# First loads on one queue in the order of need, and x turned over inside the stream of context steps

## The chip, the cores and the metric

The kernel runs on one core of a Trainium2 chip. The metric is the device time of one execution in microseconds (us), the median of several runs. The engines are TensorE (PE, matrix products and transposes; its weight loads are shown as PEld), VectorE (DVE), ScalarE (ACT), GpSimd (POOL) and SyncE (SP, which here only issues transfers). Each engine takes its instructions strictly in the order in which the program was recorded, and waits at one until what it reads is there and the buffer that it writes is free.

## The reference, cut to what matters

The program is a transformer layer with a mixer (neighbourhood attention beside a bidirectional state-space scan) and 16 experts, followed by a second layer. The change touches only the start of the first layer: the modulation of the tokens `x` (512 x 1024) and of the context `ctx` (256 x 1024), and the projection of the context that the scan needs.

```python
def _modulate(x, g, shift, scale):
    return _rmsnorm(x, g) * (1 + scale) + shift

def _ada(cvec, w_ada, b_ada):
    mod = jax.nn.silu(cvec) @ w_ada + b_ada
    return jnp.split(mod, N_MOD, axis=-1)
...
    q, k, v, z, xbc, dt_raw, gates = _split_in(h @ w_in)
    qc, kc, vc, zc, xbcc, dtc, gates_c = _split_in(hc @ w_in)
...
    xbc = jax.nn.silu(_dwconv(xbc, conv_w, conv_b))
    xs, Bm, Cm = jnp.split(xbc, [SSD_WIDTH, SSD_WIDTH + SSD_GROUPS * SSD_STATE], axis=-1)
    dt_f = jax.nn.softplus(dt_raw[..., :SSD_HEADS] + dtb_f)
```

`w_ada` is 1024 x 6144 (25 MB). Shift and scale of the first modulation are its first 2048 columns (8.4 MB); the other 4096 columns are needed later only.

## The kernel before, in words

**Start.** Two queues issue the first loads. SP issues 16 pieces of `w_ada` (tiles `aw`, 512 KB each; eight buffers, so that the last eight wait for products with the first). ACT issues constants (`ident`, `va`, `vb`), then `ctx` and `x` in pieces of 128 rows. ACT squares and sums each row block, DVE scales all six blocks, PE turns them over (transposes, `xTp`), and ACT and DVE copy the results into `cT` (context) and `xT` (tokens), all before the last products with `w_ada` (`ada`, L695). From their sum come the columns `shc` and `gsc`, and `modulate` makes the modulated context as a sum of a rounded part and a rest (`c_hi`, `c_lo`), and later the same of the tokens (`h_hi`, `h_lo`).

**The stream.** A `Stream` object (`st`) holds units of work in a queue. A unit is a block of weight columns of `w_in`. Its raw pieces are loaded by SP into two buffers `raw`; each piece is split in pairs (`wh` by ACT at L200, `wl` by DVE or POOL at L220, five pairs alive at most). A step of a unit is one row block of weights: three products (L331 to L333) per output tile. Steps are counted, and `st.defer(n, f)` records `f` once n more steps are recorded. So the number of steps, not time, fixes where a piece of work stands in each engine's order.

**The order of units.** `ub` (B of the context, 32 steps in two halves of 16), `udt` (dt, 8 steps for the context and 8 for the tokens), then four units `xc` (32 steps each, the context's part of x in groups 0 to 3), then the q/k unit. After each half of a unit ACT starts a convolution (L760), DVE does the rest of it (L765, eight instructions), and after the unit ACT applies silu and the states of the context are made (L881 turns, L890 products).

**Beside the stream.** The other 4096 columns of `w_ada` come in 16 pieces of 1 MB (`ada_load2`, issued by ACT) and are multiplied one at a time (`ada_mm2`, L911), the first `ADA0` steps in, the next every `ADA` steps. The operations of dt (`dt_ops`) are deferred one per step: a turn of `dtT` on PE (L805, tile `dtn`), a softplus by polynomial on DVE, and `sums` (L812 to L814, tile `acs`) some steps later. PSUM tiles with the tag `m` share two banks in rotation: `dtn`, `acs`, one of the two turns of a group, the state products.

Of the kernel before, what the change touches and what calls it, by code (L numbers as in the profile page):

```python
# [9 lines left out]
F32 = mybir.dt.float32  # L10
# [564 lines left out]
ADA = 10  # L575
ADA0 = 20
# [15 lines left out]
AL = 8  # L592
SX = 56
# [19 lines left out]
def first_block(kb, es, after):  # L613
# [6 lines left out]
    S.dma_start(ident, A["ident"])  # L620
# [38 lines left out]
    S.dma_start(va, A["vec_a"])  # L659
    S.dma_start(vb, A["vec_b"])  # L660
    xT = p0.tile([128, 8, T], F32, name="xT")
# [3 lines left out]
    aw = {}  # L665

    def ada_load(kh):
        for j in range(4):
            t = p00.tile([128, 2, 512], F32, tag="aw", bufs=8, name="aw")
            nc.sync.dma_start(t, A["w_ada"][256 * kh:256 * kh + 256, 512 * j:512 * j + 512].rearrange("(k p) f -> p k f", p=128))  # L670
            aw[kh, j] = t

    ada_load(0)
    ada_load(1)
    xt = p00.tile([128, 6, D], F32, name="xt")
    for t in (4, 5, 0, 1, 2, 3):
        src = A["x"][128 * t:128 * t + 128] if t < 4 else A["ctx"][128 * (t - 4):128 * (t - 4) + 128]
        S.dma_start(xt[:, t], src)
# [13 lines left out]
    def ada_mm(kh):  # L692
        for k in range(2):
            for j in range(4):
                P.matmul(ada_ps[32 * j:32 * j + 32], sil[:, 2 * kh + k], aw[kh, j][:, k],  # L695
                         start=kh == 0 and k == 0, stop=kh == 3 and k == 1, skip_group_check=True)

    ss = p0.tile([128, 6], F32, name="ss")
    junk = xT[:, 0:2].rearrange("p a b -> p (a b)")
    for t in (4, 5, 0, 1, 2, 3):  # L700
        S.activation(junk, xt[:, t], AF.Square, accum_out=ss[:, t:t + 1])
    V.tensor_scalar(ss, ss, 1.0 / D, EPS, op0=ALU.mult, op1=ALU.add)
    rs = kb.rsqrt(ss, 6, p0)
    for t in (4, 5, 0, 1, 2, 3):
        V.tensor_scalar(xt[:, t], xt[:, t], rs[:, t:t + 1], None, op0=ALU.mult)
    ada_mm(0)
    ada_load(2)
    ada_mm(1)
    ada_load(3)
    S.dma_start(tri, A["tri"])  # L710
    S.dma_start(sel, A["sel"])
    for n in range(12):
        ps = PS.bank([128, 512], F32, "gsm"[n % 3], "xTp")
        for i in range(4):
            k, t = (2 * n + i // 2, 4 + i % 2) if n < 4 else (n - 4, i)
            P.transpose(ps[:, 128 * i:128 * i + 128], xt[:, t, 128 * k:128 * k + 128], ident)
        if n < 4:
            o, v = cT[:, 2 * n:2 * n + 2].rearrange("p a b -> p (a b)"), ps
        else:
            o, v = in_time(xT[:, n - 4]), ps.rearrange("p (r g c) -> p r g c", g=8, r=8)  # L720
        if n % 2:
            V.tensor_copy(o, v)
        else:
            S.activation(o, v, AF.Copy)
    ada_mm(2)
    ada_mm(3)
# [3 lines left out]
    def modulate(v, src, hi, lo, each):  # L730
# [62 lines left out]
    def dt_ops(t0, nt):  # L793
# [14 lines left out]
        def sums():  # L808
# [24 lines left out]
               ] + [None] * (16 if t0 else 38) + [  # L833
# [4 lines left out]
    udt = Unit([([(0, A["w_in"][:, ODT:ODT + 128])], 8)], 128)  # L838
# [17 lines left out]
    kb.group_b(udt, 0, act_t, T, ev_dtx)  # L856
    udt.steps = [(0, 2 * p + r, c, f) for p, r, c, f in udt.steps]
# [68 lines left out]
    ub = xbc_unit(OB, 16, bcT, b_nat)  # L926
    st.add(udt)
    us = [xc_unit(0)]
    st.pump_some(1)
# [1785 lines left out]
```

## Time and profile before

| | |
|---|---|
| Median of 3 runs | 3428.11 us (3427.95 to 3434.9) |
| The profiled execution's own time | 3432.32 us |
| Its span in the trace | 3430.5 us |
| PE busy | 3208.5 us (94%) |
| DVE busy | 1624.5 us (47%) |
| ACT busy | 1168.1 us (34%) |
| POOL busy | 554.2 us (16%) |
| First product of the stream (L331, `ub`) | 42.02 us into the span |
| First product of the q/k unit | 154.32 us into the span |

A line of the timeline gives the start, the duration, engine and line of the kernel, the instruction with what it writes and reads, how many were merged, and in brackets how long the engine had been idle and who released it. Durations of PE are modelled, so the distance from one start to the next says more. The shares over the whole span say little here: the change lies in the first 5% of it, and what matters is which engine is waited for there.

### The profile page before, as it was taken

The numbers are of one execution on the slowest core, as the hardware profiler recorded it, in microseconds if no ns is written. First come the engines' busy times: TensorE is split into PE (matmuls) and PEld (weight loads), VectorE is DVE, ScalarE is ACT, GpSimd is POOL, SyncE is SP. The second block draws the span as 40 slices with busy tenths as digits, with TensorE's granted clock in tenths as the row PEclk, the third lists the DMA queues.
The fourth block names the chain that finished last, engine by engine and source line by source line (L and its number), as shares of the span: only waits on it lengthen the run. The fifth ranks groups of instructions, "written<-read, shape, count | busy, mean of one in ns | idle before, by whom it ended". The sixth has DMA issues, their size and how long they took to land. (4 is left out here: it accounts for less than half of the span.)

```text
span 3430.5 us, 42023 instructions
## 1 busy us (share of the span) xinstructions
PE 3208.5 (94%) x16365; PEld 2207.9 (64%) x16365; DVE 1624.5 (47%) x3113; ACT 1168.1 (34%) x2064; POOL 554.2 (16%) x371
## 2 busy tenths in 40 slices
PE   7999999999899898888889888999999999999998
PEld 4778877777678543324324224777888877788887
DVE  5745557676554410111011015776544467765444
ACT  4455545555323100100000003555433355543332
POOL 2232213444110100000000000241111103401111
PEclk9999999999999899999999999999999999999999
DMA  8622122222444799999999996212323221123232
GB/s 293 237 65 79 59 79 79 83 80 77 146 147 184 310 410 418 420 421 421 421 421 421 421 421 227 68 47 71 93 92 105 92 88 56 41 84 99 92 92 80
DMA packets 223389, 646.64 MB, mean 188 GB/s; under 512 B 17973, under 2 KB 110253, under 8 KB 171349
## 3 DMA queue, kind: packets, MB, share of 16 engines
q1 hardware_dynamic: 211176, 607.26, 46.6%
q10 hardware_dynamic: 12013, 36.69, 3.0%
q8 instruction: 129, 2.11, 0.3%
q14 instruction: 71, 0.58, 0.0%
HBM read 628.67 MB, written 15.21 MB: 188 GB/s over the span
## 5 line engine op out<-in xcount | busy, mean ns | idle before, releaser
L1968 PE MATMUL hd<-xw,xe 128*64 128x512 f32 x2048 | 462.8, 595 | 63.1 <-DMA xw<-in_w_up_dram 42.1
L220 DVE TENSOR_TENSOR wl<-raw,wh 128x1024 fp32r<-128x1024 f32 (+1 forms) x306 | 377.9, 1249 | 124.3 <-ACT wh L200 122.8
L200 ACT ACTIVATE wh<-raw 128x1024 fp32r<-128x1024 f32 (+1 forms) x349 | 343.4, 1003 | 212.2 <-PE psg L333 133.1
L331 PE MATMUL psg<-HA,wh 128*128 128x512 f32 (+1 forms) x1024 | 392.6, 383 | 0.0
L332 PE MATMUL psg<-HB,wh 128*128 128x512 f32 (+1 forms) x1024 | 387.7, 379 | 3.9 <-DVE HB L467 3.9
L333 PE MATMUL psg<-HA,wl 128*128 128x512 f32 (+1 forms) x1024 | 388.0, 379 | 0.0
L1968 PEld LDWEIGHTS hd<-xw,xe 128*64 128x64 f32 x2048 | 151.6, 137 | 363.4 <-issue 241.2
L2009 PE MATMUL down<-xw,hidT 128*64 128x512 f32 x1024 | 237.8, 600 | 36.5 <-DMA xw<-in_w_down_dram 36.4
L331 PE MATMUL psg<-h_hi,wh 128*128 128x512 f32 x584 | 255.3, 437 | 1.1 <-DVE vsb L1334 0.9
L333 PE MATMUL psg<-h_hi,wl 128*128 128x512 f32 x584 | 236.9, 406 | 0.0
L332 PE MATMUL psg<-h_lo,wh 128*128 128x512 f32 x584 | 236.5, 405 | 0.0
L332 PEld LDWEIGHTS psg<-HB,wh 128*128 128x128 f32 x1024 | 195.0, 190 | 38.6 <-DVE HB L467 4.7
L333 PEld LDWEIGHTS psg<-HA,wl 128*128 128x128 f32 x1024 | 194.6, 190 | 35.9
L331 PEld LDWEIGHTS psg<-HA,wh 128*128 128x128 f32 x1024 | 195.7, 191 | 33.8
L2009 PEld LDWEIGHTS down<-xw,hidT 128*64 128x64 f32 x1024 | 75.0, 137 | 188.1 <-issue 120.6
L2627 POOL TENSOR_TENSOR va<-va,ga 128x512 f32<-128x512 f32 x44 | 90.9, 2066 | 546.1 <-DVE va L2609 546.0
L2024 ACT ACTIVATE yh<-down,gcol 128x512 fp32r<-128x512 f32 x16 | 11.0, 686 | 489.4 <-PE down L2009 489.4
L1980 DVE TENSOR_TENSOR hid<-hid,hd 128x512 f32<-128x512 f32 x32 | 22.0, 687 | 314.0 <-PE hd L1968 313.9
L2043 POOL TENSOR_TENSOR Y<-Y,R 128x512 f32<-128x512 f32 x4 | 5.0, 1275 | 966.4 <-ACT tmp L2041 966.4
L220 POOL TENSOR_TENSOR wl<-raw,wh 128x1024 fp32r<-128x1024 f32 (+1 forms) x43 | 101.7, 2368 | 291.2 <-ACT wh L200 291.2
L331 PE MATMUL psg<-wh,hidh 128*128 128x512 f32 x352 | 139.5, 396 | 0.0
L333 PE MATMUL psg<-wh,hidl 128*128 128x512 f32 x352 | 139.2, 396 | 0.0
(487 smaller groups left out, 5979.3 us busy)
## 6 DMA issues: line engine op xcount, KB each, us to landing
xw<-in_w_gate_dram SPq DMA_DIRECT2D x128, 1024.0 KB, 19.8
xw<-in_w_up_dram SPq DMA_DIRECT2D x128, 1024.0 KB, 19.8
xw<-in_w_down_dram SPq DMA_DIRECT2D x126, 1024.0 KB, 19.8
raw<-in_w_up_dram SPq DMA_DIRECT2D x176, 256.0 KB, 3.7
raw<-in_w_in_dram SPq DMA_DIRECT2D x34, 1024.0 KB, 5.2
raw<-in_w_in_dram SPq DMA_DIRECT2D x96, 256.0 KB, 3.1
raw<-in_w_down_dram SPq DMA_DIRECT2D x44, 512.0 KB, 4.3
raw<-in_w_in_dram SPq DMA_DIRECT2D x33, 512.0 KB, 4.7
```

What stands on the lines that cost most here:

```text
L200: nc.scalar.activation(wh[:, :kn, :nco], src, AF.Copy)
L220: eng.tensor_tensor(wl[:, :kn, :nco], src, wh[:, :kn, :nco].bitcast(F32), op=ALU.subtract)
L331: nc.tensor.matmul(ps, l, r, start=first, stop=False, skip_group_check=skip)
L332: nc.tensor.matmul(ps, l, rh, start=False, stop=False, skip_group_check=skip)
L333: nc.tensor.matmul(ps, lh, r, start=False, stop=last, skip_group_check=skip)
L1968: P.matmul(ps[c][64 * e:64 * e + 64], xe[p // 2][k // 2 % 2][:, 2 * (k // 4) + k % 2, c0:c0 + 64], self.tiles[p, w, k, e][:, 512 * c:512 * ...
L1980: V.tensor_tensor(acts[p, c], acts[p, c], ps[c], op=ALU.mult)
L2009: P.matmul(down[h][64 * e:64 * e + 64], b[:, 64 * e:64 * e + 64], w[:, 1024 * r + 512 * h:1024 * r + 512 * h + 512], start=j == 0 and r == ...
L2024: S.activation(hi, down[h], AF.Copy, scale=gates[p])
L2043: G.tensor_tensor(o, o, R3[:, :512], op=ALU.mult)
L2627: G.tensor_tensor(v, v, g[j], op=ALU.mult)
```

## The change

All first loads are issued by SP in one order: constants, the two blocks of `ctx`, eight pieces of `w_ada` (now one row block of 128 x 2048 each, 1 MB, six buffers), the first two pieces of `w_in`, and only then `x`. ACT issues no loads ahead of its first work. Only the context is normalised and turned over before the stream. The tokens are squared, scaled and turned over inside the stream: squares at steps 18 to 27, the row factors at 34, the scaling at 38 to 47, and eight turns (`x_turn`) at steps 54 to 89, each with a DVE instruction that modulates straight out of PSUM. The tokens' part of dt gets a unit of its own (`udtx`, whose weights are loaded and split a second time), and stands behind `xc` of group 1 instead of behind `ub`. The other pieces of `w_ada` start 48 steps in instead of 20 and follow every 8 steps instead of 10. The context's dt is deferred by 6 steps instead of 14. Half of the rests `c_lo` go to DVE instead of POOL. Nineteen products of `ident` with itself (`warm`) stand ahead of the stream.

```diff
-ADA = 10
-ADA0 = 20
+ADA = 8
+ADA0 = 48
-AL = 8
-SX = 56
+AL = 4
+SX = 8
...
+    xt = p00.tile([128, 2, D], F32, name="xt")
+    for t in range(2):
+        nc.sync.dma_start(xt[:, t], A["ctx"][128 * t:128 * t + 128])
+    aw = []
+
+    def ada_load(k):
+        aw.append(p00.tile([128, 4, 512], F32, tag="aw", bufs=6, name="aw"))
+        nc.sync.dma_start(aw[k], A["w_ada"][128 * k:128 * k + 128, :2048].rearrange("p (j f) -> p j f", f=512))
+
+    for k in range(6):
+        ada_load(k)
...
-    for t in (4, 5, 0, 1, 2, 3):
-        S.activation(junk, xt[:, t], AF.Square, accum_out=ss[:, t:t + 1])
...
+    def x_turn(k):
+
+        ps = PS.bank([128, 512], F32, "m", "xTp")
+        for t in range(4):
+            P.transpose(ps[:, 128 * t:128 * t + 128], xx[:, t, 128 * k:128 * k + 128], ident)
+        o = cT[:, 2 * (k % 4):2 * (k % 4) + 2].rearrange("p a b -> p (a b)")
+        V.tensor_scalar(in_time(o), ps.rearrange("p (r g c) -> p r g c", g=8, r=8), gsc[:, 0, k:k + 1], shc[:, 0, k:k + 1],
+                        op0=ALU.mult, op1=ALU.add)
+        S.activation(h_hi[:, k], o, AF.Copy)
+        (G if k % 2 else V).tensor_tensor(h_lo[:, k], o, h_hi[:, k].bitcast(F32), op=ALU.subtract)
...
-            (G if k % 2 or v else V).tensor_tensor(lo[:, k], src[:, k], hi[:, k].bitcast(F32), op=ALU.subtract)
+            (G if k % 2 else V).tensor_tensor(lo[:, k], src[:, k], hi[:, k].bitcast(F32), op=ALU.subtract)
...
-               ] + [None] * (16 if t0 else 38) + [
+               ] + [None] * (16 if t0 else 22) + [
...
-        spread(14, dt_ops(4, 2) + [lambda: tt(ddc, dtv[:, 4:6], dte[:, 4:6]),
+        spread(6, dt_ops(4, 2) + [lambda: tt(ddc, dtv[:, 4:6], dte[:, 4:6]),
...
+    kb.warm("m", 14)
...
-    for i in range(3):
-        ada_load2(i)
+    st.pump_some(1)
...
-    modulate(0, xT, h_hi, h_lo, lambda k: st.fill(1.0))
-    zero.close()
+    for i in range(3):
+        st.defer(26 + 6 * i, lambda i=i: ada_load2(i))
+    rx_ = []
+    for t in range(4):
+        st.defer(18 + 3 * t, lambda t=t: S.activation(junk, xx[:, t], AF.Square, accum_out=ss[:, t:t + 1]))
+        st.defer(38 + 3 * t, lambda t=t: by_r(xx[:, t], rx_[0][:, t:t + 1]))
+    st.defer(34, lambda: rx_.append(row_r(0, 4)))
+    for k in range(8):
+        st.defer(54 + 5 * k, lambda k=k: x_turn(k))
     for g in range(1, 4):
         us.append(xc_unit(g))
+        if g == 1:
+            st.add(udtx)
         st.finish(us[g - 1])
```

**How the order moves.** On ACT, from the end of the context's rounded parts (`c_hi`) to the convolution of `ub`'s second half (the second `bcT<-psc`), before:

```order
L737 ACTIVATE c_hi<-cT 128x256 x2
L950 ACT_TABLE_LOAD
L950 ACTIVATE alog<-alog 128x64
L737 ACTIVATE h_hi<-xT 128x512 x4
L200 ACTIVATE wh<-raw 128x1024
L760 ACTIVATE bcT<-psc,cols,cw 128x256 x2
L737 ACTIVATE h_hi<-xT 128x512
...
L737 ACTIVATE h_hi<-xT 128x512
L760 ACTIVATE bcT<-psc,cols,cw 128x256 x2
```

and in the changed kernel, with line numbers of that kernel:

```order
L959 ACTIVATE alog<-alog 128x64
L200 ACTIVATE wh<-raw 128x1024
L767 ACTIVATE bcT<-psc,cols,cw 128x256 x2
L964 ACTIVATE cT,ss<-xx 128x1024
L200 ACTIVATE wh<-raw 128x1024
L964 ACTIVATE cT,ss<-xx 128x1024
L200 ACTIVATE wh<-raw 128x1024
L964 ACTIVATE cT,ss<-xx 128x1024
L911 DMA aw_430<-in_w_ada_dram 128x2048
L964 ACTIVATE cT,ss<-xx 128x1024
L200 ACTIVATE wh<-raw 128x1024
L767 ACTIVATE bcT<-psc,cols,cw 128x256 x2
```

The eight rounded parts of the tokens are gone from here, and four squares of 1024 columns stand in their place. On DVE, from the second half's convolution of group 0 (`xc`) to the copy of the sums (`acs`), in the changed kernel (before, no turn of x stands here):

```order
L220 TENSOR_TENSOR wl<-raw,wh 128x1024
L730 TENSOR_SCALAR cT<-xTp,gsc,shc 128x8x8x8
L733 TENSOR_TENSOR h_lo<-cT,h_hi 128x512
L730 TENSOR_SCALAR cT<-xTp,gsc,shc 128x8x8x8
L772 SCALAR_TENSOR_TENSOR xc<-psc,cw,xc 128x255 x2
...
L772 SCALAR_TENSOR_TENSOR xc<-psc,cw,xc 128x254 x2
L220 TENSOR_TENSOR wl<-raw,wh 128x1024
L730 TENSOR_SCALAR cT<-xTp,gsc,shc 128x8x8x8
L733 TENSOR_TENSOR h_lo<-cT,h_hi 128x512
L730 TENSOR_SCALAR cT<-xTp,gsc,shc 128x8x8x8
L822 COPY acs<-acs 128x128
```

The third L730 is the modulation of turn 4. On PE, the sums stand one bank rotation behind that turn (turn 4, turn 5, sums, all with tag `m`), with the changed kernel's rows

```order
L919 MATMUL ada<-aw_582,sil 32x512 x4
...
L728 MATMUL xTp<-ident,xx 128x128 x4
...
L728 MATMUL xTp<-ident,xx 128x128 x4
L819 MATMUL acs<-n,tri 128x2x32
L820 MATMUL acs<-n,tri 128x2x32
L821 MATMUL acs<-n,tri 128x128
```

where before the sums followed products of `xc` alone, and seven pieces of `ada` and the tokens' dt products stood ahead of them. Now four pieces do (the last of them is shown), and the tokens' dt stands behind.

## Rows read from the trace of the kernel before

**Rows 1.** Busy time by stretch: us, then PE, PEld, DVE, ACT, POOL, PEclk, DMA, GB/s
```profile
58.00:76.60 18.60, 18.60 (x128) 13.92 (x124) 17.92 (x27) 8.93 (x14) 10.64 (x5) 1.00 0.50 170
94.50:125.00 30.50, 27.57 (x194) 20.38 (x194) 25.71 (x50) 12.38 (x17) 4.75 (x2) 0.94 0.75 257
125.00:154.30 29.30, 28.65 (x201) 21.54 (x202) 22.33 (x43) 16.72 (x24) 7.36 (x4) 1.00 0.68 245
```
**Rows 2.** Timeline from the last piece of w_ada to the stream's first product
```profile
35.37 1.90 PE L695 MATMUL ada<-aw,sil 128*32 128x512 f32 x10 [1.56 <-DMA aw<-in_w_ada_dram]
39.21 1.22 DVE L220 TENSOR_TENSOR wl<-raw,wh 128x1024 fp32r<-128x1024 f32 x1 [1.21 <-ACT wh L200]
41.05 1.05 DVE L732 TENSOR_SCALAR cT<-cT,gsc,shc 128x256 f32<-128x256 f32 x3
42.02 0.58 PE L331 MATMUL psc<-c_hi,wh 128*128 128x256 f32 x1 [3.31 <-ACT c_hi L737]
```
**Rows 3.** Transfers from 0 to 60 us: GB/s in 40 slices of 1.5 us, issues
```profile
GB/s 0 124 371 358 397 408 400 400 404 403 395 407 388 385 388 385 371 388 388 388 384 392 381 385 390 310 225 410 421 437 415 354 209 4 12 232 406 49 0 5
aw<-in_w_ada_dram SPq DMA_DIRECT2D x16, 512.0 KB, 7.6
aw<-in_w_ada_dram ACTq DMA_DIRECT2D x3, 1024.0 KB, 5.0
xt<-in_ctx_dram ACTq DMA_DIRECT2D x2, 512.0 KB, 6.9
```
**Rows 4.** Timeline of ACT: squares, first convolution taps, silu with table load, weight parts
```profile
14.27 1.06 ACT L701 ACTIVATE xT<-xt 128x1024 f32<-128x1024 f32 x1
15.45 1.06 ACT L701 ACTIVATE xT<-xt 128x1024 f32<-128x1024 f32 x1
58.87 1.00 ACT L760 ACTIVATE bcT<-psc,cols,cw 128x256 f32<-128x256 f32 x2
75.74 1.28 ACT L784 ACT_TABLE_LOAD   x1 [4.12 <-DVE bcT L765]
78.00 1.99 ACT L200 ACTIVATE wh<-raw 128x1024 fp32r<-128x1024 f32 x2
```
**Rows 5.** Timeline of DVE and POOL: row factors, scalings, convolution, dt, a POOL rest
```profile
20.59 0.17 DVE L702 TENSOR_SCALAR ss<-ss 128x6 f32<-128x6 f32 x1 [12.09 <-ACT xT L701]
23.00 4.07 DVE L705 TENSOR_SCALAR xt<-xt,rs_y 128x1024 f32<-128x1024 f32 x6
66.00 4.04 DVE L732 TENSOR_SCALAR xT<-xT,gsc,shc 128x512 f32<-128x512 f32 x2
67.18 2.57 POOL L220 TENSOR_TENSOR wl<-raw,wh 128x1024 fp32r<-128x1024 f32 x1
71.70 3.96 DVE L765 SCALAR_TENSOR_TENSOR bcT<-psc,cw,bcT 128x255 f32<-128x255 f32 x8
75.58 0.41 DVE L846 COPY dtT<-psg 64x256 f32<-64x256 f32 x1
85.64 0.62 DVE L829 SCALAR_TENSOR_TENSOR d<-d,u 128x128 f32<-128x128 f32 x2
```
**Rows 6.** Timeline of PE: an ada piece, tokens' dt, turns, sums, q/k unit
```profile
66.71 1.07 PE L911 MATMUL ada<-aw,sil 128*32 128x512 f32 x8
67.70 0.49 PE L331 MATMUL psg<-h_hi,wh 128*128 128x512 f32 x1
73.55 0.28 PE L331 MATMUL psc<-c_hi,wh 128*128 128x256 f32 x1
76.59 0.33 PE L805 MATMUL dtn<-ident,dtT 64*128 64x64 f32 x2
79.08 0.60 PE L863 MATMUL bct<-ident,bcT 128*128 128x128 f32 x4
94.47 0.41 PE L812 MATMUL acs<-n,tri 128*128 128x64 f32 x2 [0.30 <-issue]
154.32 0.28 PE L331 MATMUL psg<-c_hi,wh 128*128 128x256 f32 x1
```

More of the change, by code (lines that the diff above doesn't have):

```diff
@@ L658, in first_block @@
     vb = p0.tile([120, 128], F32, name="vb")
-    S.dma_start(va, A["vec_a"])
-    S.dma_start(vb, A["vec_b"])
-    xT = p0.tile([128, 8, T], F32, name="xT")
+    nc.sync.dma_start(va, A["vec_a"])
+    nc.sync.dma_start(vb, A["vec_b"])
+    xx = p0.tile([128, 4, D], F32, name="xx")
     cT = p0.tile([128, 8, TC], F32, name="cT")
@@ L690, in first_block @@
     ada_ps = PS.bank([128, 512], F32, "o", "ada")
[L692 to L696, printed above, removed]
-    ss = p0.tile([128, 6], F32, name="ss")
-    junk = xT[:, 0:2].rearrange("p a b -> p (a b)")
-    for t in (4, 5, 0, 1, 2, 3):
-        S.activation(junk, xt[:, t], AF.Square, accum_out=ss[:, t:t + 1])
@@ L702, in first_block @@
[L702 to L709, printed above, removed]
+    ss = p0.tile([128, 6], F32, name="ss")
+    junk = cT[:, 0:4].rearrange("p a b -> p (a b)")
+    for t in range(2):
+        S.activation(junk, xt[:, t], AF.Square, accum_out=ss[:, 4 + t:5 + t])
     S.dma_start(tri, A["tri"])
@@ L711, in first_block, with row_r, by_r @@
     S.dma_start(sel, A["sel"])
-    for n in range(12):
+    def row_r(t0, n):
+        v = ss[:, t0:t0 + n]
+        V.tensor_scalar(v, v, 1.0 / D, EPS, op0=ALU.mult, op1=ALU.add)
+        return kb.rsqrt(v, n, p0)
+    def by_r(x, r):
+        V.tensor_scalar(x, x, r, None, op0=ALU.mult)
+    rc = row_r(4, 2)
+    for t in range(2):
+        by_r(xt[:, t], rc[:, t:t + 1])
+    for n in range(4):
         ps = PS.bank([128, 512], F32, "gsm"[n % 3], "xTp")
         for i in range(4):
[L715 to L718, printed above, removed]
-        else:
[L720 to L724, printed above, removed]
@@ L725, in first_block @@
-    ada_mm(2)
-    ada_mm(3)
+            P.transpose(ps[:, 128 * i:128 * i + 128], xt[:, i % 2, 256 * n + 128 * (i // 2):256 * n + 128 * (i // 2) + 128], ident)
+        o = cT[:, 2 * n:2 * n + 2].rearrange("p a b -> p (a b)")
+        if n % 2:
+            V.tensor_copy(o, ps)
+        else:
+            S.activation(o, ps, AF.Copy)
+    for k in range(8):
+        for j in range(4):
+            P.matmul(ada_ps[32 * j:32 * j + 32], sil[:, k], aw[k][:, j], start=k == 0, stop=k == 7, skip_group_check=True)
+        if k < 2:
+            ada_load(6 + k)
@@ new lines, in first_block @@
+    kb.warm("m", 5)
+    def x_turn(k):
[7 more added lines that the diff above has]
+        (G if k % 2 else V).tensor_tensor(h_lo[:, k], o, h_hi[:, k].bitcast(F32), op=ALU.subtract)
@@ L836, in dt_ops @@
         return ops
-    udt = Unit([([(0, A["w_in"][:, ODT:ODT + 128])], 8)], 128)
+    udt, udtx = (Unit([([(0, A["w_in"][:, ODT:ODT + 128])], 8)], 128) for _ in range(2))
     def spread(n0, ops, every=1):
@@ L855, in ev_dtx @@
         spread(SX, dt_ops(0, 4))
-    kb.group_b(udt, 0, act_t, T, ev_dtx)
-    udt.steps = [(0, 2 * p + r, c, f) for p, r, c, f in udt.steps]
+    kb.group_b(udtx, 0, act_t, T, ev_dtx)
+    for u in (udt, udtx):
+        u.steps = [(0, 2 * p + r, c, f) for p, r, c, f in u.steps]
     def b_nat():
@@ L950, in first_block @@
     S.activation(alog, alog, AF.Exp)
-    modulate(0, xT, h_hi, h_lo, lambda k: st.fill(1.0))
-    zero.close()
+    for i in range(3):
+        st.defer(26 + 6 * i, lambda i=i: ada_load2(i))
+    rx_ = []
+    for t in range(4):
+        st.defer(18 + 3 * t, lambda t=t: S.activation(junk, xx[:, t], AF.Square, accum_out=ss[:, t:t + 1]))
+        st.defer(38 + 3 * t, lambda t=t: by_r(xx[:, t], rx_[0][:, t:t + 1]))
+    st.defer(34, lambda: rx_.append(row_r(0, 4)))
+    for k in range(8):
+        st.defer(54 + 5 * k, lambda k=k: x_turn(k))
     for g in range(1, 4):
         us.append(xc_unit(g))
+        if g == 1:
+            st.add(udtx)
         st.finish(us[g - 1])
+        if g == 2:
+            zero.close()
     shuf = [(i + 16) % 32 for i in range(32)]
```

15 lines of the change are left out of this document (2 added, 13 removed).

## The prediction, made before the result was known

> **What bounds the kernel now.** I read the shares of the engines first, then the start of the timeline, then the stream of context steps up to the q/k unit, from where on both kernels issue the same products in the same order. So I compare one point, the first product of the q/k unit, at 154.32 us now [rows 6], and carry its shift to the end one to one.
>
> Up to 42.02 us the kernel is bound by transfers: the last piece of `w_ada` releases PE at 35.37, and the stream's first product starts at 42.02 [rows 2]. Behind that PE is nearly full, but not alone: between 58 and 77 us DVE works 17.92 of 18.60 us, and from 94.5 to 125 us 25.71 of 30.50 [rows 1]. The reader should see two engines close to full in one stretch. Whichever gets more work there, or work in a worse order, sets the pace. From 94.5 us to the q/k unit PE idles only 2.93 and 0.65 us [rows 1].
>
> **The loads.** Ahead of the last piece of `w_ada` now stand 8.4 MB of `w_ada` itself (16 x 512 KB), 1.05 MB of context [rows 3], and some 0.4 MB of constants, 9.8 MB in all; the 2.1 MB of `x` are behind. The steady rate is 0.39 MB/us, and 0.41 to 0.44 in the slices that carried the 1 MB pieces with long rows [rows 3], which is the form all of `w_ada` now has. With 2.3 us before anything moves that is 25.7 to 27.5 us; I take 26.3. Before, the first product came 6.65 us behind that piece. Now the next thing needed is the first weight piece, 1.05 MB or 2.5 us later; then its ACT part (1.0, half of the 1.99 in [rows 4]) and its DVE rest (1.22), which the order puts ahead of the scaling; then 0.97 us from scaling to product as now (41.05 to 42.02) [rows 2]. The `ada` sum, its copy and the columns run beside the weight piece. First product: 26.3 + 2.5 + 0.1 + 1.0 + 1.2 + 1.0 = 32.1, a head start of 9.9 us (8.7 to 10.5 by the two rates).
>
> **The first unit.** Its first half still goes by the weight pairs: DVE rest 1.2, scaling 0.4, rounded part 0.4, next ACT part 1.0 make about 3.1 each, so the last `c_hi` is done at about 42.0, and PE finishes the half near 43.6. The `warm` products stand in a wait and cost nothing; without that cover they would be 19 x 0.15 (0.60 for four in [rows 6]) = 2.9.
>
> **ACT behind it.** In the changed order ACT has, in a row from 42.0: table load 1.3, one small activation 0.2, a weight part 1.0, two taps 1.0, four squares at 1.18 (14.27 to 15.45) and three weight parts between them, then the tap of the second half 0.5 [rows 4]. That is 11.7, so 53.7. DVE, which waits for the third of these weight parts, then does the second half's convolution (3.96 in [rows 5]) to 58.2, the twelve small row-factor operations 2.4 (20.59 to 23.00), the first scaling of x 0.7 (4.07 for six), and only then the copy of `dtT`, 0.4 [rows 5]: 61.7. The context's dt turn on PE needs that copy. Counting a step as 0.35 us (24 products of twice the width take 73.55 minus 67.70 [rows 6], so half of 0.24 per product, three products), PE would be there at 43.6 + 5.6 + 2.8 + 1.8 = 53.8. **It waits 8 us**, and every product of `xc` group 0 from its sixth step on is queued behind it. Before, the turn stood at 76.59, behind 14 instead of 6 steps, four `ada` pieces and the tokens' dt [rows 6], which covered the same lag of DVE.
>
> **DVE from 61.7 to turn 4.** It goes on alone. ACT: table and silu behind the convolution (1.28 + 1.0), a weight part 1.0; POOL takes the rest of it to about 64.0 (2.57 [rows 5]), and DVE's next rest finishes at 65.2. Three scalings of x 2.0, eight dt operations at 0.3 (0.62 for two [rows 5]), one of them longer, 3.1: 70.3. Turn 0: modulation 0.65, waiting for its rounded part 0.65, rest 0.65 (512 columns, between the 0.41 of 256 and the 1.22 of 1024 [rows 2, 5]); two dt 0.5; the convolution 4.0; three dt 0.8; turn 1 0.65; four dt 1.2: 79.3. Then DVE waits for two weight parts behind two other copies on ACT, and for POOL, to 82.7; rest 1.2, turn 2 with its wait and rest 2.0, turn 3 0.6: 86.5. Waits 1.1, convolution 3.9: 91.5. Table, silu, weight part on ACT 3.3; rest 1.2; **turn 4 is out of its bank at 96.7.** The sums `acs` on PE reuse that bank, so they start at 96.8; now they start at 94.47 [rows 6]. The head start is gone, and PE is 2.3 us late.
>
> Two of those waits, 2.4 us together, are for POOL. The rows: two scalings of 512 columns took 4.04 beside POOL's 2.57, while six twice as wide took 4.07 without it [rows 5]. The Trainium skill says so as a rule (SBUF — State Buffer, "Who interferes with whom"): a DVE instruction with two SBUF inputs, or in a fast mode, and a GpSimd instruction exclude each other for the whole instruction. The trace agrees for these scalings; without exclusion the sum below would be 6.8 instead of 9.2.
>
> **What is left behind the sums.** Before, 59.85 us from the sums to the q/k unit (94.47 to 154.32 [rows 6]). Now three more `ada` pieces stand there (12 of 16 instead of 9) at 1.2 (1.07 and the restart), the tokens' dt 5.85, and two turns at 0.45 (the 0.60 of four transposes less their overlap) [rows 6]: 3.6 + 5.85 + 0.9 = 10.35. Before lost 2.93 + 0.65 us idle there and 1.8 to a clock of 0.94 over 30.5 us [rows 1], 5.4 together. The tokens' dt now lies where the longest of these waits was (a weight rest behind silu) and covers it; I expect one new wait of 2.0, the tokens' `dtT` copy behind a convolution. So 3.4 is won.
>
> **Sum.** 2.3 + 10.35 - 3.4 = 9.2 us later at the q/k unit. The profiled execution took 3432.32 in all for a span of 3430.5, so it would become 3441.5; it stands 4.2 above the median of 3428.11, inside the spread of the three runs. From the median: 3437.3. The extra load and split of the dt weights (one piece of 0.5 MB, one pair) is in the DVE and ACT queues above and hidden behind PE's 5.85.
>
> **Rivals.**
> - *PE sets the pace from the first product on* (faster). If DVE and ACT keep within their buffers, the head start of 9.9 stays, the first unit gains 1.0, the eight turns cost 3.6: 7.3 faster, 3420.8. For it: DVE is not full in the present kernel (4.8 us idle from 94.5 to 125, 7.0 from there to 154.3 [rows 1]). Against it: the order puts 11.7 us of ACT and then 7 of DVE ahead of one copy. It decides at the dt turn: if that starts before 56 us, this rival holds.
> - *The same chain, shorter by some 5 to 9 us.* Waits at turns 2 and 4 (3.4 and 3.3 for ACT) may be less if ACT runs ahead: 0 to 4 us later, about 3430.5. No row shows turn instructions straight from PSUM with a scale; they could cost 0.5 or 1.0 (half of the wider rest, or the whole), which is 0.8 less or 1.8 more over five of them.
> - *The transfers do not gain.* If 1 MB pieces on one queue move at 0.36, the first value behind the start [rows 3], the last `w_ada` piece lands at 29.5 and everything is 3 us later: 3440.5.
> - *The clock.* The granted clock is 0.94 in the stretch in which PE idles 2.93 us, 1.00 in the others [rows 1]: behind a wait PE runs for a while at the lower of its levels, 1.2 instead of 2.4 GHz. A fall after the sums costs 1.8 more: 3439. It is within the forecast's own range, and the Trainium skill (TensorE: Matmul & The Clock Gate, "What's actually happening") gives the same direction, idleness bringing back the lower level.
>
> **How the numbers follow.** The forecast (6 to 13 us later) has 0.48 with the clock's case in it, the shorter chain 0.30, the slow transfers 0.08, PE's pace 0.14. A change of 0.2% or 6.9 us is about what a measurement of this kernel can tell from none, so slower means above 3435.0. Of the forecast 0.40 lie above it and 0.08 below, the slow transfers above: 0.48 slower. The shorter chain and that 0.08 make the same, with a fifth of PE's pace: 0.40. Faster: 0.12. The forecast's own range is 3434 to 3442; for 8 in 10 I reach down to 3422 and up to 3446 (forecast, slow transfers and a fall of the clock together).
>
> **What would show it.** The first product at 31 to 33.5 us; the context's dt turn near 62 with an idle time of several us released by DVE; the sums near 97 released by DVE (turn 4); the q/k unit near 163. Wrong if PE has few waits between 44 and 97 us, if the sums come before 91, or if DVE's rests and scalings do not wait for POOL.

## The result and the profile after

| | before | after |
|---|---|---|
| Median | 3431.12 us (4 runs, 3427.95 to 3434.9) | 3461.95 us (4 runs, 3461.24 to 3462.57) |
| Ratio, 95% interval | 1 | 1.0087 [1.0076, 1.0099] |
| Span of the profiled execution | 3430.5 us | 3460.2 us |
| First product of the stream | 42.02 us | 35.62 us |
| Context's dt turn (`dtn`) | 76.59 us | 65.80 us |
| Sums (`acs`) | 94.47 us | 101.54 us |
| First product of the q/k unit | 154.32 us | 175.52 us |
| From there to the end | 3276.2 us | 3284.7 us |

The change makes the kernel 31 us slower by the medians (30 by the ratio), where 9 were forecast from the three runs of the kernel before that were known then (median 3428.11). The stream starts 6.4 us earlier, is 7.1 us late at the sums, 21.2 us late at the q/k unit, and loses another 8.5 us behind it, where the prediction had carried the shift one to one.

The stretches of the changed kernel, in the columns of [rows 1]:

```profile
35.60:56.50 20.90, 17.63 (x138) 16.34 (x136) 12.41 (x22) 15.40 (x26) 8.61 (x6) 1.00 0.64 214
56.50:66.00 9.50, 0.47 (x5) 0.27 (x3) 7.86 (x23) 5.17 (x7) 0.18 (x1) 0.66 0.64 227
66.00:101.60 35.60, 24.12 (x169) 18.70 (x168) 26.15 (x46) 13.81 (x20) 9.49 (x5) 0.84 0.58 200
101.60:130.00 28.40, 24.39 (x153) 18.15 (x153) 18.88 (x33) 12.48 (x18) 8.25 (x4) 0.90 0.62 222
130.00:175.50 45.50, 43.75 (x298) 31.68 (x299) 27.76 (x53) 19.78 (x26) 9.61 (x4) 0.96 0.70 238
```

Before, PE was nearly full and DVE close behind. Now no engine is full between 56 and 130 us: from 66.0 to 101.6 PE works 24.12 of 35.60 us, DVE 26.15, ACT 13.81. Where no engine is full, they wait for one another in turn. The waits of PE from the first product to the q/k unit (who waited for whom, us in total, times, longest):

```profile
PE dtn L812 <- DVE dtT L853: 9.0, 1, 9.0
PE acs L819 <- DVE cT L730: 8.2, 1, 8.2
PE ada L919 <- DVE modx L922: 4.3, 1, 4.3
PE xTp L728 <- DVE cT L730: 3.2, 1, 3.2
PE psc L332 <- DVE c_lo L745: 3.2, 3, 1.1
PE acs L819 <- ACT hc L900: 1.4, 1, 1.4
```

They sum to 29.3 us. The same list of the kernel before sums to 7.5 us behind its first product. The start, answering [rows 2]:

```profile
27.94 1.93 PE L719 MATMUL ada<-aw,sil 128*32 128x512 f32 x8 [0.59 <-DMA aw<-in_w_ada_dram]
29.80 2.50 PE L311 MATMUL warm<-ident 128*128 128x128 f32 x10
31.72 1.06 ACT L200 ACTIVATE wh<-raw 128x1024 fp32r<-128x1024 f32 x1 [16.43 <-DMA raw<-in_w_in_dram]
32.09 0.65 PE L941 MATMUL ptm<-ident,mod 128*128 128x128 f32 x4
33.49 1.22 DVE L220 TENSOR_TENSOR wl<-raw,wh 128x1024 fp32r<-128x1024 f32 x1
35.62 0.36 PE L331 MATMUL psc<-c_hi,wh 128*128 128x256 f32 x1
```

The last piece of `w_ada` lands at 27.9 us (26.3 forecast), the first weight piece at 31.7, 3.8 us behind it and not 2.5. Now the dt turn, on the timeline of all engines:

```profile
56.16 1.06 ACT L200 ACTIVATE wh<-raw 128x1024 fp32r<-128x1024 f32 x1 [1.61 <-DMA raw<-in_w_in_dram]
57.13 1.00 ACT L767 ACTIVATE bcT<-psc,cols,cw 128x256 f32<-128x256 f32 x2
58.40 3.98 DVE L772 SCALAR_TENSOR_TENSOR bcT<-psc,cw,bcT 128x255 f32<-128x255 f32 x8
65.33 0.41 DVE L853 COPY dtT<-psg 64x256 f32<-64x256 f32 x1
65.80 0.47 PE L812 MATMUL dtn<-ident,dtT 64*128 64x64 f32 x2 [9.03 <-DVE dtT L853]
```

PE arrives at 56.8 us and stands until DVE has done a convolution and the row factors. The tap (57.13) stands on ACT behind a weight part that waited for its transfer until 56.16: that wait of 1.61 us, unlike the squares, had no place in the forecast. And the sums:

```profile
92.15 3.98 DVE L772 SCALAR_TENSOR_TENSOR xc<-psc,cw,xc 128x255 f32<-128x255 f32 x8 [1.61 <-ACT xc L767]
96.21 1.28 ACT L791 ACT_TABLE_LOAD   x1 [4.09 <-DVE xc L772]
97.50 1.06 ACT L791 ACTIVATE xc<-xc 128x1024 f32<-128x1024 f32 x1
98.47 1.04 ACT L200 ACTIVATE wh<-raw 128x1024 fp32r<-128x1024 f32 x1
99.54 1.23 DVE L220 TENSOR_TENSOR wl<-raw,wh 128x1024 fp32r<-128x1024 f32 x1 [3.41 <-ACT wh L200]
100.68 0.81 DVE L730 TENSOR_SCALAR cT<-xTp,gsc,shc 128x512 f32<-128x512 f32 x1
101.54 0.69 PE L819 MATMUL acs<-n,tri 128*128 128x64 f32 x2 [8.24 <-DVE cT L730]
```

Read it from below: the sums need the bank that turn 4 holds; its modulation (0.81 us) stands on DVE behind a weight rest, this behind a weight part on ACT, this behind silu and its table, these behind the whole convolution. An operation of 0.8 us inherits 8.5 us of others (92.15 to 100.68).

### The profile page after: what moved, and what is told of

It reads as the page before. It is cut to its first block, busy times and chain, and to the rows that moved or that the text cites. A ratio compares the mean times of both kernels' runs of the same rounds, so it can differ in the third digit from the quotient of the medians.

```text
span 3460.2 us, 42097 instructions
## 1 busy us (share of the span) xinstructions
PE 3219.7 (93%) x16403; PEld 2218.9 (64%) x16403; DVE 1619.7 (47%) x3127; ACT 1170.1 (34%) x2063; POOL 546.1 (16%) x366
## 5 line engine op out<-in xcount | busy, mean ns | idle before, releaser
L220 DVE TENSOR_TENSOR wl<-raw,wh 128x1024 fp32r<-128x1024 f32 (+1 forms) x308 | 387.2, 1271 | 127.7 <-ACT wh L200 126.4
```

Source lines behind the costliest of these rows:

```text
L220: eng.tensor_tensor(wl[:, :kn, :nco], src, wh[:, :kn, :nco].bitcast(F32), op=ALU.subtract)
```

## The experiments

Each run was measured beside the kernel before on one chip, and its ratio is to that one, whose median lay between 3430.3 and 3432.9 us. So where two runs differ by a few us, the ratios say more than the medians. The times of the places come from each run's profile; "rest" is from the q/k unit to the end.

```
                          median us  ratio to before          first product, dt turn, sums, q/k unit, rest
after                      3461.95   1.0087 [1.0076, 1.0099]  35.62  65.80  101.54  175.52  3284.7
rotation kept              3455.12   1.0074 [1.0061, 1.0087]  35.42  65.14  100.92  175.14  3281.4
before, rotated            3441.10   1.0030 [1.0018, 1.0042]  41.97  76.54   94.54  156.74  3282.7
ada pieces early           3461.76   1.0091 [1.0077, 1.0105]  34.94  69.45  105.18  176.02  3281.5
turns 4 to 7 later         3464.31   1.0100 [1.0084, 1.0116]  35.64  66.11   92.70  175.22  3284.7
dt turn later              3468.88   1.0107 [1.0093, 1.0121]  36.30  69.44  108.52  182.69  3284.5
no warm                    3460.65   1.0085 [1.0071, 1.0099]  35.36  64.37  100.14  173.88  3284.3
no normalisation           3463.41   1.0091 [1.0076, 1.0107]  35.66  64.68  101.82  175.46  3287.5
before, loads only         3430.48   1.0001 [0.9993, 1.0010]  41.94  76.54   94.45  153.70  3273.7
tap first                  3467.40   1.0100 [1.0085, 1.0116]  35.81  70.04  105.86  179.40  3287.4
no turns                   3448.58   1.0051 [1.0038, 1.0064]  35.61  67.39   87.18  160.99  3284.0
three edits                3459.44   1.0079 [1.0067, 1.0092]  35.16  69.41  104.61  177.91  3279.7
before, w_in first         3433.88   1.0003 [0.9994, 1.0012]  41.51  76.08   94.03  153.28  3278.5
no turns, rotation kept    3441.80   1.0026 [1.0015, 1.0037]  35.09  66.92   86.42  160.45  3279.9
turns on ACT               3458.88   1.0078 [1.0064, 1.0091]  35.18  64.86   95.72  170.49  3285.1
ada 4 steps earlier        3454.54   1.0070 [1.0058, 1.0082]  34.86  64.76  100.61  168.35  3283.0
all four edits             3443.61   1.0032 [1.0020, 1.0044]  34.76  63.86   94.33  160.06  3282.0
```

**The rest behind the q/k unit.** Every second weight rest goes to POOL, by the running number of the pair. `udtx` adds one pair, so from group 2 on POOL has the rests that DVE had, and the other way round, in the whole remainder of the first block. Two runs change that alone, one in each direction:

```diff
-    eng = nc.gpsimd if self.pool_share and self.pair_i % self.pool_share == 0 else nc.vector
+    eng = nc.gpsimd if self.pool_share and (self.pair_i + self.by * (self.pair_i > self.cut)) % self.pool_share == 0 else nc.vector
# rotation kept
+    st.cut, st.by = 13, -1
# before, rotated
+    st.cut, st.by = 12, 1
```

> The changed kernel, but the extra pair of dt weights (udtx) is not counted where the program decides by turns whether POOL or DVE makes a weight rest; from the q/k unit on, both engines then have the same rows as in the kernel before. In the two profiles the stretch from the q/k unit to the end takes 3276.2 us before and 3284.7 after. Rotation theory: those 8.5 us are this shift of the turns, so the stretch is back at 3276 to 3278 and the time falls to about 3454. Rival (they are scatter between two executions, or a late start that grows by itself): the stretch stays at 3283 to 3286 and the time at 3460 to 3463.

> The kernel before, with the turns of POOL and DVE at the weight rests shifted by one from the context group 2 on, and nothing else. Rotation theory: the stretch from the q/k unit to the end takes 3283 to 3286 instead of 3276 and the time is about 8 us above the kernel before (3439 beside 3431). Rival (scatter): within 2 us of the kernel before.

Measured: the first is 6.8 us faster than the changed kernel by the medians and 4.5 by the ratios, whose intervals just overlap; the second is 10.8 us slower than the kernel before, 10.3 by the ratio, and 2.4 us of this have arisen by the q/k unit. The lists of PE's waits between the q/k unit and 1160 us have the same fingerprint in the two kernels with the shifted turns. Four lines of each list, from the changed kernel, and from the kernel before with the turns shifted:

```profile
PE psg L331 <- ACT wh L200: 7.5, 2, 6.6
PE psg L333 <- POOL wl L220: 2.6, 2, 1.9
PE stp L1410 <- POOL xd L1399: 1.9, 2, 1.1
PE psg L331 <- DVE xs L772: 1.7, 1, 1.7
```
```profile
PE psg L332 <- ACT wh L201: 7.7, 2, 6.8
PE psg L334 <- POOL wl L221: 2.5, 2, 1.9
PE stp L1392 <- POOL xd L1381: 2.1, 2, 1.4
PE psg L332 <- DVE xs L767: 1.5, 1, 1.5
```

In the kernel before and in the changed one with the old turns, the last three do not appear among the waits of over 1 us, and the first is 5.0 and 6.1 us. So the rotation costs time, in both directions; the run "no turns, rotation kept" below adds a third value, 8.6 us by the ratios, with intervals that do not overlap. But it does not explain the whole 8.5 us behind the q/k unit: the rest of "rotation kept" is 3281.4 us, between the rotation theory (3276 to 3278) and the rival. The profiles of all runs show how much it explains. The 8.5 us arise between the q/k unit and the first product of the experts' router (tile `lg`): that stretch took 960.3 us before and 970.8 after, and what follows it 2315.9 and 2313.9.

```
q/k unit to the router's first product           us               mean    waits of PE in it, us
stream of the kernel before (3 profiles)     957.8 to 960.3    959.0       21.5 to 23.4
the same, turns shifted (1)                       965.2                    27.7
changed stream, old turns (4)                963.2 to 966.2    964.3       25.0 to 26.9
changed stream, shifted turns (10)           965.9 to 970.8    967.9       28.2 to 30.8
```

The last two ranges touch, but PE's waits in them do not. By the means, the shifted turns cost 3.6 of 9.0 us there in the changed stream, and 6.2 in the stream of the kernel before. Some 5 us stay when the turns are put back, and no run shows what causes them.

**Work on x, and the turns.** Three runs take parts of it away or move it:

```diff
# no normalisation; no turns
-    rx_ = []
-    for t in range(4):
-        st.defer(18 + 3 * t, lambda t=t: S.activation(junk, xx[:, t], AF.Square, accum_out=ss[:, t:t + 1]))
-        st.defer(38 + 3 * t, lambda t=t: by_r(xx[:, t], rx_[0][:, t:t + 1]))
-    st.defer(34, lambda: rx_.append(row_r(0, 4)))
# no turns, besides
-    for k in range(8):
-        st.defer(54 + 5 * k, lambda k=k: x_turn(k))
+    st.defer(2, lambda: [G.memset(h.bitcast(F32), 0.0) for h in (h_hi, h_lo)])
# turns 4 to 7 later
-        st.defer(54 + 5 * k, lambda k=k: x_turn(k))
+        st.defer(54 + 5 * k + 14 * (k > 3), lambda k=k: x_turn(k))
```

> The changed kernel with the tokens left unnormalised: four squares on ACT (4.9 us), twelve row-factor operations (2.4) and four scalings (2.8) on DVE are left out; the turns of x stay. Work theory (they lie on the chain to the dt turn and to the sums): the copy of dtT comes at 62.3 instead of 65.3 and the sums up to 5.2 us earlier, so 3457 to 3459. Rival (the chain waits for the weight piece at 56.2 us and for convolution, silu and rests, and the squares are hidden): only the 3.1 us of DVE ahead of the copy are won, and half of them is lost again at the weight rest that follows it (66.7): 3460 to 3461.

> The changed kernel, with the turns 4 to 7 of x 14 steps later, behind the sums. The wait of 8.24 us ahead of the sums is for the bank that turn 4 holds. Bank theory: without turn 4 in front of them the sums start at about 93.5 instead of 101.5 and most of the 8 us is won (3454 to 3457). Queue theory: PE is held by DVE and ACT anyway, because the next weight rest stands behind convolution, silu and weight part at 99.5 us; the wait then moves to a product behind the sums, which needs that rest at 100.8, and no more than 2 us are won (3460 to 3462).

> The changed kernel without the work on the tokens in the stream: squares, row factors, scalings and the eight turns with their modulation are left out, and h_hi and h_lo are set to zero once; the products with them stay. Turn theory (DVE's modulation of a turn stands behind a convolution and holds up ACT and PE; normalisation alone costs nothing): the waits of 3.24 and 8.24 us at turn 2 and at the sums go, with 3.6 us of PE work: the sums at 88 to 93 us, the q/k unit at 161 to 166, time 3448 to 3453. Rival (the chain of convolution, silu and weight rests sets the pace by itself, with or without turns): the sums at 97 to 101, the q/k unit at 170 to 174, time 3457 to 3461.

Leaving out 10 us of ACT and DVE work on the normalisation won nothing in the time (the rival's 3460 to 3461 is nearer than the work theory, and too low as well). ACT, relieved of the squares, only issues a piece of `w_ada` 2 us earlier (49.39 instead of 51.42), and the weight piece that the last part ahead of the tap waits for arrives later; this run's timeline of ACT:

```profile
58.10 1.06 ACT L200 ACTIVATE wh<-raw 128x1024 fp32r<-128x1024 f32 x1 [7.04 <-DMA raw<-in_w_in_dram]
59.06 1.00 ACT L767 ACTIVATE bcT<-psc,cols,cw 128x256 f32<-128x256 f32 x2
```

That weight piece is issued at 49.87 us (49.83 in the changed kernel), once POOL's rest of 47.4 has freed its buffer, and now lies behind a piece of `w_ada` and not ahead of it. The 7 us of idle time say that ACT is not short of time there. But this run does not show that the normalisation costs nothing, because the weight piece is now 1.94 us later (58.10 and not 56.16) and takes the convolution and silu behind it along. On DVE something was won: the twelve row-factor operations and the first scaling (3.1 us) stood between convolution and copy, and three scalings behind the next rest. In spite of the later piece the dt turn comes 1.1 us earlier (64.68), and the modulation of turn 0 only 0.28 later (73.88 in the changed kernel); this run's DVE:

```profile
60.33 3.97 DVE L772 SCALAR_TENSOR_TENSOR bcT<-psc,cw,bcT 128x255 f32<-128x255 f32 x8
64.22 0.41 DVE L853 COPY dtT<-psg 64x256 f32<-64x256 f32 x1
74.16 0.81 DVE L730 TENSOR_SCALAR cT<-xTp,gsc,shc 128x512 f32<-128x512 f32 x1
```

What leaving it out would win with the weight piece in its old place was not tried. With turns 4 to 7 behind the sums, these start at 92.70 as the bank theory says, and the time does not fall, as the queue theory says (2 us above its range). The wait moves, but not to a weight rest: PE waits again for a bank that a turn's modulation on DVE frees, now at a turn of `xn` at 109.43, by this run's list of waits:

```profile
PE dtn L812 <- DVE dtT L853: 9.3, 1, 9.3
PE xn L889 <- DVE cT L730: 5.2, 1, 5.2
PE ada L919 <- DVE modx L922: 4.9, 1, 4.9
```

Without the turns, the sums come at 87.18, the q/k unit at 160.99, and 13.4 us are won (12 by the ratios), as the turn theory says. Only 3.6 of them are PE's own work (an estimate: eight turns at 0.45, as in the forecast); the rest is waiting that goes with the turns. The two places tried for turns 4 to 7 cannot be told apart in time.

**Which queue the turns hold.** The modulation moved to ACT, the rests to POOL:

```diff
-        V.tensor_scalar(in_time(o), ps.rearrange("p (r g c) -> p r g c", g=8, r=8), gsc[:, 0, k:k + 1], shc[:, 0, k:k + 1],
-                        op0=ALU.mult, op1=ALU.add)
+        S.activation(in_time(o), ps.rearrange("p (r g c) -> p r g c", g=8, r=8), AF.Identity, scale=gsc[:, 0, k:k + 1], bias=shc[:, 0, k:k + 1])
-        (G if k % 2 else V).tensor_tensor(h_lo[:, k], o, h_hi[:, k].bitcast(F32), op=ALU.subtract)
+        G.tensor_tensor(h_lo[:, k], o, h_hi[:, k].bitcast(F32), op=ALU.subtract)
```

> The changed kernel with the modulation of the eight turns on ACT (scale and shift in one activation out of PSUM) and all their rests on POOL; DVE has no part in the turns. DVE-queue theory (the 3.24 and 8.24 us are waits for a bank that DVE's modulation frees only behind a convolution of 4 us): the waits at turn 2 and the sums fall to under 3 us together, the sums come at 93 to 96, time 3451 to 3456. Rival (ACT's queue has silu in the same place, which waits for the same convolution, and weight parts behind it): the sums stay at 99 to 103, time 3459 to 3464.

Between the two: the wait at turn 2 is gone and the q/k unit comes 5.0 us earlier, but the wait at the sums stays, with the same chain on another engine:

```profile
91.70 1.28 ACT L790 ACT_TABLE_LOAD   x1 [7.73 <-DVE xc L771]
93.00 1.06 ACT L790 ACTIVATE xc<-xc 128x1024 f32<-128x1024 f32 x1
93.96 1.04 ACT L200 ACTIVATE wh<-raw 128x1024 fp32r<-128x1024 f32 x1
94.91 0.76 ACT L730 ACTIVATE cT<-xTp,shc,gsc 128x512 f32<-128x512 f32 x1
```
```profile
95.72 0.69 PE L818 MATMUL acs<-n,tri 128*128 128x64 f32 x2 [8.59 <-ACT cT L730]
```

So it is not DVE's queue but its convolution that is waited for; ACT's silu waits for it too, and whatever stands behind silu.

**The order around the dt turn.** Three runs:

```diff
# dt turn later
-        spread(6, dt_ops(4, 2) + [lambda: tt(ddc, dtv[:, 4:6], dte[:, 4:6]),
+        spread(14, dt_ops(4, 2) + [lambda: tt(ddc, dtv[:, 4:6], dte[:, 4:6]),
# tap first
-    st.wait = WAIT
+    st.wait = 16
+    st.defer(34, lambda: setattr(st, "wait", WAIT))
# ada pieces early
-ADA = 8
-ADA0 = 48
+ADA = 10
+ADA0 = 20
-        st.defer(26 + 6 * i, lambda i=i: ada_load2(i))
+        ada_load2(i)
```

> The changed kernel, with the context's dt deferred by 14 steps as in the kernel before, and not by 6. PE now waits 9.03 us at that turn while weight pair 1 and 2 of the group xc 0 are ready at 55.7 and 58.5 us. One-to-one theory (the order of PE around the turn sets everything behind it): seven steps, 2.5 us, move into the wait, and as DVE's convolutions follow PE, the sums and the end come 2.5 us earlier: about 3459.5. Rival (PE waits for the weight rest behind silu anyway, at 68.2 us): the wait falls and another appears at products within the next ten steps, the end moves by less than 1 us: 3461 to 3463.

> The changed kernel, where a weight pair is split 16 instead of 14 steps behind its load during the first 34 steps. On ACT the fourth weight part behind alog, the one that waits for its transfer until 56.16 us, then stands behind the second tap and silu instead of ahead of the tap. Transfer theory (this late piece, and not the work on x, holds the dt turn): the tap is done at 55 instead of 57.6, and the convolution, the copy of dtT and the dt turn come 2.5 to 3.5 us earlier (62.3 to 63.3 instead of 65.8); what follows carries it, 3458 to 3460. Rival (the chain behind convolution, silu and weight rests holds PE): the dt turn comes earlier but PE waits at a product for the weight pair that is now later, and the sums stay at 101 to 102 us: 3461 to 3463.

> The changed kernel, with the other pieces of w_ada as in the kernel before: first product 20 steps in, then every 10 steps, the first three loads issued before the stream. Filling theory: three more pieces stand ahead of the sums, in time in which PE waits anyway (9.0, 3.2 and 8.2 us), so about 3.6 us less stand behind them, and the wait of 4.35 us for the copy of the first half (modx) goes too: 3454 to 3458. Rival (the transfers collide): three pieces of 1 MB ahead of weights and x delay the weight pieces of the first 20 us of the stream by up to 7 us, the dt turn starts later than 65.8, and the time stays or rises (3462 to 3468).

The first two missed on both sides: 7 and 5 us slower. (With the later dt turn the first states of group 0 read factors that are made only behind them; the amount of work is the same.) With the later dt turn PE waits ahead of it for a weight part (4.5 us, as the rival says) and no longer at it, but the operations of dt on DVE then lie among the turns of x: PE waits 12.3 us in all for modulations and 9.7 for `modx`. With the tap first, the tap comes at 54.82 and the convolution ends at 59.8, as planned, but the weight parts now stand behind silu, and on DVE the row factors and the copy of `dtT` stand behind the weight rest that waits for them; this run's DVE and POOL:

```profile
63.24 1.23 DVE L220 TENSOR_TENSOR wl<-raw,wh 128x1024 fp32r<-128x1024 f32 x1 [3.41 <-ACT wh L200]
64.38 2.31 DVE L699 TENSOR_SCALAR ss<-ss 128x4 f32<-128x4 f32 x1
69.57 0.41 DVE L853 COPY dtT<-psg 64x256 f32<-64x256 f32 x1
```
```profile
64.23 2.43 POOL L220 TENSOR_TENSOR wl<-raw,wh 128x1024 fp32r<-128x1024 f32 x1 [9.04 <-ACT wh L200]
```

The copy comes 4.2 us later than in the changed kernel. With the pieces early the rival's range is met (3461.76), and a weight piece is late: ACT waits 3.43 us for a weight piece at 52.03, the dt turn comes at 69.45, and the 3.1 us won behind the sums (70.8 from there to the q/k unit, and not 74.0) are lost in front of them.

**The later order, the warm products, and edits together.**

```diff
# ada pieces 4 steps earlier
-ADA0 = 48
+ADA0 = 44
# no warm products
-    kb.warm("m", 5)
...
-    kb.warm("m", 14)
```

> The changed kernel with the other pieces of w_ada 4 steps earlier (44 instead of 48). Piece 8 waits 4.35 us at 126 us for the copy of the first half's sum (modx), which stands on DVE behind a weight rest that follows convolution and silu; 4 steps earlier that copy stands ahead of the convolution. Queue theory: the wait goes, and 3 to 4 us with it: 3458 to 3459. Rival: PE waits for the same convolution, silu and weight rest at the next product: 3461 to 3463.

> The changed kernel without its 19 warm products. In its trace ten records of them stand between the last ada product (27.94) and the turn of the columns (32.09), at a granted clock of 0.5. Cost theory: the turn of the columns starts at 30.7, the columns are ready when the first weight part is (32.8), and the stream's first product comes at 35.0 instead of 35.62; 0.6 us are won in all, 3461.3. Rival (they hold the clock up): without them the clock stays at its lower level beyond 32.5 us, the first products run at the lower level, and the end is 1 to 3 us later: 3463 to 3465.

> The changed kernel with three edits together: POOL's turns at the weight rests as in the kernel before, no warm products, and the fourth weight part behind the second tap. If their gains add up (6.8 and 1.3 us measured, 0 to 4 expected): 3450 to 3454. If the waits only move: 3454 to 3456. By both it stays above the kernel before, whose products of the q/k unit start 20 us earlier.

> The changed kernel without the work on the tokens in the stream (h_hi and h_lo set to zero once, as in the run without turns), and with POOL's turns at the weight rests as in the kernel before. If the two causes are independent, their gains add: 3448.6 less 7 is 3441 to 3442, and what is left to the kernel before, 9 to 11 us, is the new order of the stream itself (dt turn early, tokens' dt and more pieces of w_ada behind the sums). If the rotation only shifted the same waits: 3446 to 3449.

> The changed kernel with POOL's turns at the weight rests as before, no warm products, the turns' modulation on ACT with all rests on POOL, and the pieces of w_ada 4 steps earlier. If each gains what it is given alone (7, 1.3, 6 to 10, 3 to 4): 3440 to 3445; if turns and copy only move the waits: 3452 to 3455. Above the kernel before by both.

Four steps earlier, the pieces of `w_ada` give 7.4 us by the medians (5.8 by the ratios), more than expected: the wait for `modx` is gone, and one piece now fills part of the wait at the dt turn (4.2 us left of 9.0). Without the warm products 1.3 us are won by the medians and 0.7 by the ratios, which is within the scatter. The last three show that the causes add up, roughly. By the medians the sums agree to 0.3 us: tap first, rotation and warm, +5.4 - 6.8 - 1.3, give 3459.2 from 3461.95, measured 3459.44; no turns and rotation 3441.8, measured 3441.80; all four edits, -6.8 - 1.3 - 3.1 - 7.4, 3443.4, measured 3443.61. That closeness is luck, as the kernel before was itself up to 2.6 us slower beside some of these runs than beside others. By the ratios the three gain 2, 4 and 5 us more than the sum of their parts, which their intervals allow. What the run without turns and with the old rotation still has above the kernel before is 8.9 us (3432.91 in that comparison). It comes from the new order of the stream: 6.1 us at the q/k unit (160.45 and not 154.32), the others behind it. Its largest waits ahead of the q/k unit are 7.2 us at the dt turn and 3.7 for a state's copy. How the parts of the new order share the 8.9 was not separated.

**The loads alone.** In the kernel before, only the load side of the change; and then with the first piece of `w_in` between those of `w_ada`:

```diff
# both (eight pieces of w_ada behind ctx and x, all loads on one queue)
-        S.dma_start(xt[:, t], src)
+        nc.sync.dma_start(xt[:, t], src)
...
+        aw.append(p00.tile([128, 4, 512], F32, tag="aw", bufs=4, name="aw"))
+        nc.sync.dma_start(aw[k], A["w_ada"][128 * k:128 * k + 128, :2048].rearrange("p (j f) -> p j f", f=512))
# w_in first, besides
+        if k == 1:
...
+            nc.sync.dma_start(st.early[0], A["w_in"][:512, OB:OB + 512].rearrange("(k p) f -> p k f", p=128))
```

> The kernel before, with the load side of the change alone: one queue (SP) in the order constants, context, x, eight pieces of w_ada of 1 MB (four buffers), then w_in; x is still normalised and turned over before the stream, and the stream is that of the kernel before. Load theory: 11.95 MB in front of w_in at the rate of the changed kernel (9.8 MB in 25.6 us behind 2.3, and 0.42 for the further 2.1) bring the last w_ada piece at 32.9 instead of 35.4, and the stream's first product at 39.6 to 40.7 instead of 42.0: 1.3 to 2.4 us are won, 3429. Rival (DVE's and ACT's work on x then sits ahead of the columns, because x comes no earlier): the first product stays at 42 or later and the time at 3431 to 3434.

> The kernel before with the load side alone, as in the run of that name, and with the first weight piece of w_in loaded between the pieces of w_ada. In that run the piece released ACT at 38.04 us, 5 us behind the last piece of w_ada, and the columns stood behind its rest on DVE. Theory: with the piece there early, the last piece of w_ada ends at 35.5 and the first product follows the columns, at 39.5 to 40 instead of 41.94; 2 us are won, 3428. Rival: DVE and ACT then hold the first unit anyway, and nothing is won, 3430 to 3431.

Both rivals hold: by the ratios (1.0001 and 1.0003) nothing is won. In the first run the first product comes at 41.94 and in the second at 41.51; the first run's line:

```profile
41.94 0.58 PE L331 MATMUL psc<-c_hi,wh 128*128 128x256 f32 x1 [5.33 <-ACT c_hi L732]
```

So neither the one queue nor the larger pieces give the 6.4 us of head start by themselves. What is left is that the 2.1 MB of x and its work stand behind; that alone was not tried. No version tried beats the kernel before.

## Why the prediction came out as it did

The direction was right and the size was not: 3437.3 forecast, 3461.95 measured, outside both ranges (3434 to 3442, and 3422 to 3446). The marks up to the sums came within 5 us, and none of the three signs of being wrong that the prediction names came about. They all lie ahead of the sums; most of the miss lies behind. Against its own marks:

```
                 forecast   measured   behind the forecast by
first product      32.1       35.62      3.5
dt turn            61.7       65.80      4.1
sums               96.8      101.54      4.7
q/k unit          163.5      175.52     12.0
end (span)       3439.7     3460.2      20.5
```

- **The loads** (a term mis-sized by 3.5). The weight piece came 3.8 us behind the last `w_ada` piece where 2.5 were counted, that piece 1.6 later than forecast, and from the weight piece to the product it took 3.9 where 3.3 were counted. "The `warm` products stand in a wait and cost nothing" was right as far as the runs can tell.
- **The dt turn** (right in place and size, in part by luck). PE waited 9.03 us where 8 were forecast, and the turn is far above the 56 us from which the rival "PE sets the pace" would have held. The row on ACT that was put at 11.7 us had 11.7 us of work, but took 13.3 (44.80 to 58.13), since it also waited 1.61 us for a weight piece; that wait was not in the sum. Two terms that were too large hide it in part: from the first product to the last `c_hi` it took 9.2 us (9.9 counted), and from the tap to the copy of `dtT` 7.6 (8.0 counted). With the weight piece that late, the squares did not set the end of the row. The row factors and the first scaling on DVE did stand ahead of the copy, as forecast.
- **DVE to turn 4** (right). From the dt turn to the sums 35.7 us against 35.1, released by DVE's modulation of turn 4, and not by errors that cancel: the modulations of turns 0 and 1 start 3.6 and 3.7 us behind the sum's own marks, turn 4's end 4.8. That DVE waits for POOL was right too: the rest at 66.73 took 2.55 us beside POOL's of 65.82 to 68.19, and the one at 85.64 took 2.07, against 1.23 at 57.25, and this is the exclusion that the Trainium skill describes (SBUF — State Buffer, "Who interferes with whom").
- **Behind the sums** (mis-sized by 7.3). "I expect one new wait of 2.0, the tokens' `dtT` copy behind a convolution": that wait did not come. Two others did, 4.35 us at `modx` and 1.42 at the tokens' sums. And the sum took off the 1.8 us that the kernel before loses to the clock [rows 1] as if nothing would take their place; the granted clock was 0.90 over 28.4 us and 0.96 over 45.5, which costs at most 4.7 us (0.10 by 28.4 and 0.04 by 45.5). The waits are 3.8 over the forecast, and the clock up to 4.7: enough for the 7.3. The forecast named the clock as a rival of 1.8 and did not add it.
- **"Carry its shift to the end one to one"** (the step that failed, 8.5). That both kernels "issue the same products in the same order" from the q/k unit on is true of PE, and was taken to be true of the rest. The extra pair of `udtx` was priced by its own work, "in the DVE and ACT queues above"; what it also does is shift the turns of POOL and DVE at every later weight rest. The runs show that this costs some 4 us of the 8.5 (6 in the stream of the kernel before); the cause of the others stays open.

By removal, one behind the other and by the ratios, the 30 us are: 12 for the turns of x in the stream, 9 for the rotation, and 9 for the new order of the stream (with the head start already taken off). The rotation taken by itself gave 4.5 in the changed kernel and 10 in the kernel before, so these shares hold to a few us only.

## What to carry to other kernels

Where work is dealt out by turns (every second one to another engine), a change that adds or removes one item shifts everything behind it: compare the order of all engines to the end of the program before carrying a shift one to one. Price a moved step by what it will stand behind in its new queue: a modulation of 0.8 us came out 8 us late behind a convolution, silu and weight parts, on DVE and on ACT alike. And before a piece of work is given a price on the critical chain, ask what else the next instruction in its queue waits for: the four squares (4.9 us) ended ahead of a weight part that had to wait for its transfer anyway. Taking work out can also start a transfer earlier and another one later, so read the run's trace before calling the work free.

## What the runs showed of the hardware

A DVE instruction on 4 columns took 2.31 us in the run with the tap first (0.16 us in the changed kernel), while POOL's weight rest of 64.23 to 66.66 was running, and ended with it, at 66.69: what makes DVE wait for POOL holds up the smallest instruction too. The warm products did hold the clock up, without a gain in time. The changed kernel, and then the one without them, in the columns of [rows 1]:

```profile
36.00:44.00 8.00, 5.49 (x36) 4.55 (x36) 6.43 (x12) 4.57 (x8) 2.14 (x3) 1.00 0.52 182
```
```profile
36.00:44.00 8.00, 6.95 (x36) 6.29 (x36) 6.43 (x11) 4.33 (x8) 1.91 (x3) 0.73 0.58 201
```

The granted clock was 1.00 with them and 0.73 without, and the same 36 products took 5.49 and 6.95 us; but in that stretch PE waits for DVE's rests (`c_lo`), so the slower products fit into the waits. And the transfer engines were 0.89 busy at 299 GB/s from 28 to 32 us in the changed kernel, while the first weight piece arrived, against 406 and 416 GB/s in the 4 us on either side; why that piece moves more slowly was not tried.
